# A decoder layer on one core: the feed-forward's first part cut into 6 and 10 blocks, copies issued by k-tiles

## The chip, the core and the metric

The kernel runs on one core of a Trainium2 chip. The metric is the device time of one execution in microseconds (us). Before the change it is 1711.41 us, the median of three runs (1711.17 to 1711.67).

## What is computed

One layer of a hybrid decoder for 256 prompt positions and 8 x 4 sample positions, 288 columns in all, with a model width of 2048 and a feed-forward width of 5632, in float32. Cut to the part in question:

```python
x1 = _layernorm(ALPHA * x + mixed @ w_out, ln1_g, ln1_b)

a, b = jnp.split(x1 @ w_up, 2, axis=-1)
a, conv_ffn_new = _causal_dwconv(a, conv_ffn_prev, w_conv_ffn)
y = _layernorm(ALPHA * x1 + (jax.nn.silu(a) * b) @ w_down, ln2_g, ln2_b)
```

Ahead of it stand one large input projection, a gated convolution, windowed attention over the prompt and over key/value caches, and two branch projections. The caches are also outputs: most of their rows are copied unchanged from input to output.

## The kernel before, in words

Features lie on the partitions in blocks of 128, the 288 positions in the columns. Every product is 128 output features by 288 positions, summed over k-tiles of 128 inputs. Operands are split into a high and a low float32r part, and a k-tile takes three matmuls (lines 245 to 247): high weight by high input, high weight by low input, low weight by high input. A product over 16 k-tiles has 48 matmuls.

`product` (its text is below) takes the next weight block from `w_ready` and calls `prepare` for the one after it. `prepare` loads a block of `weight_list` into `wst` (three buffers) by a DMA on SP's queue, and `half_block` splits it by eight k-tiles at a time: ACT casts to `whi`, DVE subtracts to `wlo` (four buffers each, line 251). Behind some loads it issues `copy_rest`, one of 84 copies of cache rows, 1 MB each, from input to output; before the change behind loads 20, 23, 27, 30, ..., that is 3 in 10 loads. The scheduler orders the instructions of every engine by a simulation of its own when the program is built.

The feed-forward runs over three parts of 16, 16 and 12 blocks (`THIRDS`). For each block k of a part there are two products with the input x: the first (`pa`) goes through the convolution (`conv_in`, `conv` at line 775) and silu (line 1083), the second (`pb`) is multiplied onto it (`gated`, lines 798 to 803), and the result is split into `gh[:, k]` and `gl[:, k]` (tiles `yah` and `yal`). Then 16 products of the part's own k-tiles with `w_down` follow, whose results are added into `dd`, the residual.

Part 0 is special. When it starts, the mean and the deviation of the first layer norm are only just known, so x still holds the values before normalising, times the gain. Its products therefore take `x_gb`, x with two more columns that carry gain and offset (290 columns), and `normed` (lines 1052 to 1055) finishes each result with the deviation `n1.r` and with `n1.nmr`. Beside it, in each of its 16 blocks, one of the 16 blocks of `dd` is normalised: two instructions on POOL (lines 1097 and 1098) and one on ACT (line 1099), held behind that block's `last_rows` (lines 787 and 788). In part 0's down-projection each `dd` block is split anew into x (`xh`, `xl`), then multiplied by ALPHA and added to the product (line 1116). From part 1 on x is normalised, and the products take 288 columns.

Of the kernel before, what the change touches and what calls it, by code (L numbers as in the profile page):

```python
# [12 lines left out]
AF = mybir.ActivationFunctionType  # L13
ALU = mybir.AluOpType
# [3 lines left out]
P = 128  # L18
D = 2048
KD = D // P  # L20
# [11 lines left out]
KF = FF // P  # L32
HK = KD // 2
THIRDS = (16, 16, 12)
NG, NH = 3, 4
DIL = (1, 4, 16)
BAND = 128
# [65 lines left out]
def layer_kernel(ctx: ExitStack, tc: tile.TileContext, ins, outs):  # L103
# [34 lines left out]
        return ap.bitcast(F32)  # L138


    loads = [0]
    w_load = [None]
    steps_on = [False]
    no_sync = mybir.DependencyInfo(mybir.DependencyClass.NoSync, mybir.DependencyReason.DATA)
# [9 lines left out]
    def copy_rest(after):  # L154
        if copies:
            behind(sp.dma_start(*copies.pop()), after)
# [10 lines left out]
    def weight_list():  # L167
        for b in range(3, NB_QKV + 3 * KD):
            yield ins["w_in"][b], KD
        for gate, w, nk in ((0, "w_a", KD), (KD, "w_b", NH)):  # L170
            for i in range(KD):
                yield ins["w_in"][NB_QKV + 3 * KD + gate + i], KD
                yield ins[w][i], nk
        for i in range(KD):
            yield ins["w_out"][i], KD
        f = wd = 0
        for nf in THIRDS:
            for _ in range(2 * nf):
                yield ins["w_up"][f], KD
                f += 1  # L180
            for _ in range(KD):
                yield ins["w_down"][wd : wd + nf * P * P].rearrange("(p c) -> p c", p=P), nf
                wd += nf * P * P

    w_left = weight_list()

    def prepare():
        src, nk = next(w_left, (None, 0))
# [6 lines left out]
        for k0 in range(0, nk, HK if loads[0] == 1 else nk):  # L195
            k = slice(k0, k0 + (HK if loads[0] == 1 else nk))
            d = sp.dma_start(st[:, k, :], src[:, k])
        n = loads[0]
        w_load[0] = d
        if n >= 20 and n % 10 in (0, 3, 7):  # L200
            copy_rest(d)
        w_ready.append([half_block(st, k0, min(HK, nk - k0)) for k0 in range(0, nk, HK)])

    last_mm = [None]
# [855 lines left out]
    f = 0  # L1060
# [3 lines left out]
    ident_r = sb(big, [P, P], "v_s", F32R)  # L1064
    act.copy(ident_r, ident)
    sums = []
    for part, nf in enumerate(THIRDS):
        gh = sb(big, [P, KD, T], "yah", F32R)
        gl = sb(big, [P, KD, T], "yal", F32R)
        for k in range(nf):  # L1070
# [18 lines left out]
                gated(gf, y, pb)  # L1089
            last_split = split(gh[:, k], gl[:, k], gf)  # L1090
            f += 1
            if part == 1:
                next(factors, None)
            if part == 0:

                with tc.issue_after(i_rows.ins):
                    pool.tensor_tensor(dd[:, k], dd[:, k], n1.r, ALU.mult)
                    pool.tensor_tensor(dd[:, k], dd[:, k], n1.nmr, ALU.add)
                act.activation(dd[:, k], dd[:, k], AF.Identity, bias=n1.at(n1.b, k), scale=n1.at(n1.g, k))
        if f == KF:  # L1100
            sp.dma_start(outs["o_cf"].rearrange("p (k r) -> p k r", k=KF), cf)
        if f == KF:
# [218 lines left out]
```

## Time and profile before

| | |
|---|---|
| median of three runs | 1711.41 us |
| the profiled execution: span from first to last instruction | 1709.3 us |
| the median of the runs less that span | 2.1 us |
| PE busy | 1700.4 us (99%) |
| DVE busy | 1194.6 us (70%) |
| ACT busy | 939.0 us (55%) |
| POOL busy | 387.1 us (23%) |
| DMA mean rate | 255 GB/s |

A time of its own beside the span is not listed for the profiled execution; it is one of the program's executions, and the runs stand 2.1 us above its span. The busy times say how long an engine had at least one instruction under way; a matmul counts with its whole way through the array, so that neighbours overlap. Part 0's up-projection runs from about 917 to 1105 us, its down-projection to about 1199.

### The profile page before, as it was taken

To read this page: it belongs to the slowest core of one execution; us is meant where nothing else is said; L and a number is where in the kernel's file an instruction comes from. 1 tells how busy PE (TensorE), PEld (TensorE's weight loads), DVE (VectorE), ACT (ScalarE), POOL (GpSimd) and SP (SyncE) were. 2 spreads that over 40 slices of the span, in tenths; PEclk is the share of its full clock that TensorE was granted. 3 is DMA by queue.
4 is the path that set the end of the run, shared out by engine and by line. 5 is a ranking of instruction groups with operands and counts; after the bars stand their busy time and mean duration, and the time that the engine had idled before them with its cause. 6 is when DMAs were issued, how large, how long until landed. Compare 5 with 4: busy or idle time off the path is not lost.

```text
span 1709.3 us, 34306 instructions
## 1 busy us (share of the span) xinstructions
PE 1700.4 (99%) x14138; PEld 1695.1 (99%) x14138; DVE 1194.6 (70%) x1575; ACT 939.0 (55%) x1657; POOL 387.1 (23%) x507
## 2 busy tenths in 40 slices
PE   9999999999999999999999999999999999999998
PEld 9999999999999999999999999999999999999997
DVE  5577898978887765455788887855686554555575
ACT  5578886645566564444546555543555443344454
POOL 1123332202222120011453332300111100011164
PEclk9999999999999999999999999999999999999999
DMA  8787886667778886677766666665666666666663
GB/s 295 289 299 311 333 320 251 227 260 278 268 290 341 319 313 248 225 255 258 273 232 227 230 246 227 232 233 222 228 232 256 222 231 237 247 224 234 218 243 133
DMA packets 59212, 436.16 MB, mean 255 GB/s; under 512 B 7664, under 2 KB 11504, under 8 KB 19312
## 3 DMA queue, kind: packets, MB, share of 16 engines
q1 hardware_dynamic: 57616, 429.85, 67.6%
q10 hardware_dynamic: 1440, 4.13, 0.7%
q8 instruction: 110, 1.80, 0.4%
q14 instruction: 46, 0.38, 0.1%
HBM read 427.50 MB, written 94.53 MB: 305 GB/s over the span
## 4 chain that ended last, share of the span: by engine, by line
PE 99%; DVE 0%; DMA 0%; ACT 0%; SPq 0%; issue 0%; DVEq 0%; ACTq 0%
PE acc L245 32%; PE acc L247 32%; PE acc L246 32%; PE acc L333 1%; PE att L478 0%; DMA wst<-in_w_in 0%; PE acc L437 0%; DVE yah L983 0%; PE att L597 0%; DVE ybh L957 0%; PE att L893 0%; PE att L896 0%; ACT cache L954 0%; DVE cache L965 0%; DVE cache L966 0%; DVE cache L989 0%
## 5 line engine op out<-in xcount | busy, mean ns | idle before, releaser
L251 DVE TENSOR_TENSOR wlo<-wst,whi 128x1024 fp32r<-128x1024 f32 (+1 forms) x578 | 739.5, 1282 | 404.0 <-ACT whi L251 401.1
L251 ACT CAST whi<-wst 128x1024 fp32r<-128x1024 f32 (+1 forms) x578 | 588.9, 1021 | 689.0 <-PE acc L246 613.4
L245 PE MATMUL acc<-xh,whi 128*128 128x288 f32 (+1 forms) x3216 | 921.1, 286 | 0.0
L246 PE MATMUL acc<-xl,whi 128*128 128x288 f32 (+1 forms) x3216 | 920.3, 286 | 0.0
L247 PE MATMUL acc<-xh,wlo 128*128 128x288 f32 (+1 forms) x3216 | 920.3, 286 | 0.0
L245 PEld LDWEIGHTS acc<-xh,whi 128*128 128x128 f32 x3216 | 607.8, 189 | 1.4 <-issue 1.4
L247 PEld LDWEIGHTS acc<-xh,wlo 128*128 128x128 f32 x3216 | 607.8, 189 | 0.0
L246 PEld LDWEIGHTS acc<-xl,whi 128*128 128x128 f32 x3216 | 607.8, 189 | 0.0
L247 PE MATMUL acc<-yah,wlo 128*128 128x288 f32 x1216 | 347.7, 286 | 0.0
L246 PE MATMUL acc<-yal,whi 128*128 128x288 f32 x1216 | 347.7, 286 | 0.0
L245 PE MATMUL acc<-yah,whi 128*128 128x288 f32 x1216 | 347.6, 286 | 0.0
L246 PEld LDWEIGHTS acc<-yal,whi 128*128 128x128 f32 x1216 | 229.8, 189 | 0.0
L247 PEld LDWEIGHTS acc<-yah,wlo 128*128 128x128 f32 x1216 | 229.8, 189 | 0.0
L245 PEld LDWEIGHTS acc<-yah,whi 128*128 128x128 f32 x1216 | 229.8, 189 | 0.0
L787 POOL COPY qk_s<-u 128x2 f32<-128x2 f32 x44 | 36.9, 838 | 535.2 <-ACT u L1080 412.5
L775 DVE SCALAR_TENSOR_TENSOR cy<-u,prm,cy 128x304 f32<-128x304 f32 x120 | 72.8, 606 | 6.0 <-ACT cy L773 2.8
L562 POOL TENSOR_TENSOR cache<-cache,dd 128x1024 f32<-128x1024 f32 x16 | 34.0, 2126 | 93.1 <-DMA cache<-in_cv 93.1
L251 ACT CAST yah<-ya 128x288 fp32r<-128x288 f32 x76 | 32.6, 429 | 24.4 <-DVE ya L803 8.2
L562 POOL TENSOR_TENSOR cache<-cache,qk_s 128x1024 f32<-128x1024 f32 x16 | 32.1, 2013 | 54.8 <-DMA cache<-in_ck 51.4
L768 POOL COPY u<-prm 128x16 f32<-128x16 f32 x60 | 43.1, 719 | 4.6 <-DMA prm<-in_prm 4.6
L846 POOL TENSOR_TENSOR ya<-ya,dd 128x288 f32<-128x288 f32 x16 | 13.7, 856 | 133.8 <-DVE ya L845 132.9
L560 ACT ACTIVATE cache<-cache,qk_s 128x128 f32<-128x128 f32 x128 | 40.7, 391 | 0.0
(230 smaller groups left out, 1187.2 us busy)
## 6 DMA issues: line engine op xcount, KB each, us to landing
wst<-in_w_in SPq DMA_DIRECT2D x112, 1024.0 KB, 5.1
wst<-in_w_up SPq DMA_DIRECT2D x88, 1024.0 KB, 4.9
wst<-in_w_down SPq DMA_DIRECT2D x32, 1024.0 KB, 4.9
cache<-in_ck SPq DMA_DIRECT2D x18, 1024.0 KB, 7.9
cache<-in_cv SPq DMA_DIRECT2D x18, 1024.0 KB, 8.7
wst<-in_w_a SPq DMA_DIRECT2D x16, 1024.0 KB, 5.4
wst<-in_w_out SPq DMA_DIRECT2D x16, 1024.0 KB, 5.0
wst<-in_w_down SPq DMA_DIRECT2D x16, 768.0 KB, 4.4
```

What stands on the lines that cost most here:

```text
L245: pe.matmul(out, hi[:, c, :], xh_k, start=k == 0, stop=False)
L246: pe.matmul(out, hi[:, c, :], xl_k, start=False, stop=False)
L247: last_mm[0] = pe.matmul(out, lo[:, c, :], xh_k, start=False, stop=k == nk - 1)
L251: return act.copy(hi, src), dve.tensor_tensor(lo, src, f32(hi), ALU.subtract)
L333: i = pe.matmul(o[b], first_w(term == 2, b, k), xk, start=k == 0 and term == 0, stop=k == KD - 1 and term == 2,)
L560: behind(act.activation(o[:, a, b], t[:, a, b], AF.Copy, scale=w[:, a, b : b + 1]), w_split[0])
L562: behind(pool.tensor_tensor(o, t, w.unsqueeze(3).broadcast_to([P, *n]), ALU.mult), w_split[1])
L768: pool.tensor_copy(tail[:, :, 0:2], prm[:, state : state + 2 * NB].rearrange("p (b r) -> p b r", b=NB))
L775: dve.scalar_tensor_tensor(y, u[:, i : i + YW], prm[:, w0 + i : w0 + i + 1], y, ALU.mult, ALU.add)
L787: pool.tensor_copy(dst[:, 0:2], u[:, SEQ : SEQ + 2])
L846: pool.tensor_tensor(m, m, ma[:, i], ALU.add)
```

## The change

`PARTS` has four entries: which third of `w_down`, its first k-tile in that third, and the number of blocks. The first third of 16 blocks is done as 6 and then 10. The weight arrays stay as they are laid out; a down-projection load of the first two parts takes 6 or 10 of a row's 16 k-tiles. In the first part, which is now of 6 blocks, each block normalises two or three blocks of `dd` (2, 3, 3, 2, 3, 3). The steps of the second norm's factors stay with the 16 blocks of the second third (`part == 2`). `copy_rest` is now called when 49 k-tiles have been loaded since the last copy, counted from load 20 on.

```diff
+PARTS = (0, 0, 6), (0, 6, 10), (1, 0, 16), (2, 0, 12)
+N_COPY = 49
...
-        f = wd = 0
-        for nf in THIRDS:
+        f = 0
+        for third, k0, nf in PARTS:
             for _ in range(2 * nf):
                 yield ins["w_up"][f], KD
                 f += 1
+            n = THIRDS[third] * P
+            wd = sum(THIRDS[:third]) * KD * P * P
             for _ in range(KD):
-                yield ins["w_down"][wd : wd + nf * P * P].rearrange("(p c) -> p c", p=P), nf
-                wd += nf * P * P
+                block = ins["w_down"][wd : wd + n * P].rearrange("(p c) -> p c", p=P)
+                yield block[:, k0 * P : (k0 + nf) * P], nf
+                wd += n * P
...
-        n = loads[0]
         w_load[0] = d
-        if n >= 20 and n % 10 in (0, 3, 7):
-            copy_rest(d)
+        if loads[0] >= 20:
+            to_copy[0] += nk
+            if to_copy[0] >= N_COPY:
+                to_copy[0] -= N_COPY
+                copy_rest(d)
...
-    for part, nf in enumerate(THIRDS):
+    for part, (_, _, nf) in enumerate(PARTS):
...
-            if part == 1:
+            if part == 2:
                 next(factors, None)
             if part == 0:
-                with tc.issue_after(i_rows.ins):
-                    pool.tensor_tensor(dd[:, k], dd[:, k], n1.r, ALU.mult)
-                    pool.tensor_tensor(dd[:, k], dd[:, k], n1.nmr, ALU.add)
-                act.activation(dd[:, k], dd[:, k], AF.Identity, bias=n1.at(n1.b, k), scale=n1.at(n1.g, k))
+                for i in range(k * KD // nf, (k + 1) * KD // nf):
+                    with tc.issue_after(i_rows.ins):
+                        pool.tensor_tensor(dd[:, i], dd[:, i], n1.r, ALU.mult)
+                        pool.tensor_tensor(dd[:, i], dd[:, i], n1.nmr, ALU.add)
+                    act.activation(dd[:, i], dd[:, i], AF.Identity, bias=n1.at(n1.b, i), scale=n1.at(n1.g, i))
```

The built program shows what this moves. At the end of part 0's last block, ACT had in a row before (the lines of the changed kernel are 10 or 11 higher):

```order
L1083 ACTIVATE cy_13503<-cy_13503 128x304
L1099 ACTIVATE dd_10045<-dd_10045,prm_182 128x288
L251 CAST whi_13645<-wst_13643 128x1024
L251 CAST yah_11185<-ya_13567 128x288
L251 CAST xh_91<-dd_10045 128x2x144
```

and has now:

```order
L261 CAST whi_12168<-wst_12166 128x768
L1062 COPY wgb_12091<-acc_12041 128x2
L1093 ACTIVATE cy_12030<-cy_12030 128x304
L1110 ACTIVATE dd_10044<-dd_10044,prm_182 128x288 x3
L261 CAST yah_11184<-ya_12090 128x288
L261 CAST xh_91<-dd_10044 128x2x144 x3
L261 CAST whi_12196<-wst_12194 128x768
```

The last cast into `yah` has three instructions on `dd` ahead of it, where it had one, and the cast of the fourth down block's weights moved ahead of all.

On POOL the same block had one pair:

```order
L787 COPY qk_s_11181<-u_13491 128x2
L788 COPY qk_s_11181<-u_13491 128x16
L1097 TENSOR_TENSOR dd_10045<-dd_10045,cache_10046 128x288
L1098 TENSOR_TENSOR dd_10045<-dd_10045,cache_10046 128x288
L766 MEMSET u_14783 128x2
```

and has three, all first halves ahead of all second halves:

```order
L797 COPY qk_s_11180<-u_12018 128x2
L798 COPY qk_s_11180<-u_12018 128x16
L1108 TENSOR_TENSOR dd_10044<-dd_10044,cache_10045 128x288 x3
L1109 TENSOR_TENSOR dd_10044<-dd_10044,cache_10045 128x288 x3
L776 MEMSET u_12761 128x2
```

On PE the first down products of part 0 now begin with 15 matmuls (five k-tiles) each of `acc_12116`, `acc_12144` and `acc_12172`; then the fourth product and the first use of the sixth k-tile stand so:

```order
L255 MATMUL acc_12200<-yah_11184,whi_12168 128x288
L256 MATMUL acc_12200<-yal_11185,whi_12168 128x288
L255 MATMUL acc_12116<-yah_11184,whi_12037 128x288
L255 MATMUL acc_12144<-yah_11184,whi_12112 128x288
L255 MATMUL acc_12172<-yah_11184,whi_12140 128x288
L257 MATMUL acc_12200<-yah_11184,wlo_12169 128x288
L256 MATMUL acc_12116<-yal_11185,whi_12037 128x288
L257 MATMUL acc_12116<-yah_11184,wlo_12038 128x288
```

Ahead of the first row are six more matmuls of `acc_12200`, so that 53 matmuls precede the first that reads the last block of `yah`. Before, that place came behind 45 matmuls of the first down product and 12 of the second.

## Rows read from the trace of the kernel before

**Rows 1.** The page: busy time, share of the span, instructions; granted clock in 40 slices.

```profile
PE 1700.4 (99%) x14138; PEld 1695.1 (99%) x14138; DVE 1194.6 (70%) x1575; ACT 939.0 (55%) x1657; POOL 387.1 (23%) x507
PEclk9999999999999999999999999999999999999999
```

**Rows 2.** The waits of PE: us in total, times, longest.

```profile
PE acc L263 <- DVE cy L260: 1.2, 1, 1.2
PE att L996 <- DVE ybh L957: 0.6, 1, 0.6
PE acc L333 <- ACT whi L300: 0.4, 1, 0.4
PE acc L978 <- DVE yah L983: 0.4, 1, 0.4
```

**Rows 3.** Windows of 160 us: busy us and (count) of PE, PEld, DVE, ACT, POOL.

```profile
940.00:1100.00 160.00, 160.00 (x1300) 160.00 (x1299) 131.06 (x192) 93.69 (x163) 54.23 (x81) 1.00 0.64 232
1210.00:1370.00 160.00, 160.00 (x1309) 160.00 (x1308) 112.02 (x193) 82.07 (x136) 22.91 (x55) 1.00 0.64 234
```

**Rows 4.** Timeline of PE, the first matmul of the first down product: start, us.

```profile
1105.37 0.29 PE L245 MATMUL acc<-yah,whi 128*128 128x288 f32 x1
```

**Rows 5.** Timeline of POOL in the last block of part 0.

```profile
1104.04 0.79 POOL L787 COPY qk_s<-u 128x2 f32<-128x2 f32 x1 [7.69 <-ACT u L1077]
1104.93 1.14 POOL L1097 TENSOR_TENSOR dd<-dd,cache 128x288 f32<-128x288 f32 x1
1106.15 0.92 POOL L1098 TENSOR_TENSOR dd<-dd,cache 128x288 f32<-128x288 f32 x1
1107.05 1.16 POOL L768 COPY u<-prm 128x16 f32<-128x16 f32 x1
```

**Rows 6.** Timeline of ACT there.

```profile
1107.10 0.63 ACT L1099 ACTIVATE dd<-dd,prm 128x288 f32<-128x288 f32 x1 [0.19 <-POOL dd L1098]
1110.01 0.43 ACT L251 CAST yah<-ya 128x288 fp32r<-128x288 f32 x1 [0.57 <-DVE ya L803]
```

**Rows 7.** Timeline of DVE there.

```profile
1106.53 1.62 DVE L251 TENSOR_TENSOR wlo<-wst,whi 128x1024 fp32r<-128x1024 f32 x1
1108.07 0.45 DVE L1054 TENSOR_TENSOR h<-acc,cache 128x288 f32<-128x288 f32 x1
1108.55 0.52 DVE L1055 SCALAR_TENSOR_TENSOR h<-cache,wgb,h 128x288 f32<-128x288 f32 x1
1109.18 0.49 DVE L800 SCALAR_TENSOR_TENSOR ya<-h,wgb,cy 128x256 f32<-128x256 f32 x1
1109.58 0.39 DVE L803 SCALAR_TENSOR_TENSOR ya<-h,wgb,cy 128x16 f32<-128x16 f32 x2
```

**Rows 8.** Groups by shape on DVE, 930 to 1112, then 1300 to 1410.

```profile
L775 DVE SCALAR_TENSOR_TENSOR cy<-u,prm,cy 128x304 f32<-128x304 f32 x32 | 25.6, 801 | 2.0 <-ACT cy L773 0.3
...
L775 DVE SCALAR_TENSOR_TENSOR cy<-u,prm,cy 128x304 f32<-128x304 f32 x16 | 8.5, 532 | 0.3
```

**Rows 9.** Line 1097 on POOL: duration ns, min/median/max, first and last start.

```profile
L1097 POOL TENSOR_TENSOR dd<-dd,cache x16: 792/1132/1139, 930.3 to 1104.9; 128x288 f32<-128x288 f32 x16
```

**Rows 10.** Groups by shape in part 0's down-projection, 1112 to 1200: DVE, then ACT.

```profile
L251 DVE TENSOR_TENSOR wlo<-wst,whi 128x1024 fp32r<-128x1024 f32 x30 | 36.8, 1225 | 26.3 <-ACT whi L251 26.3
L1116 DVE SCALAR_TENSOR_TENSOR dd<-dd,acc 128x288 f32<-128x288 f32 x16 | 7.3, 454 | 12.6 <-PE acc L247 12.6
L251 DVE TENSOR_TENSOR xl<-dd,xh 128x288 fp32r<-128x288 f32 x15 | 6.8, 454 | 0.0
...
L251 ACT CAST whi<-wst 128x1024 fp32r<-128x1024 f32 x31 | 32.4, 1046 | 52.4 <-PE acc L246 52.4
```

**Rows 11.** The page: DMA issues, count, KB each, median us to landing.

```profile
wst<-in_w_down SPq DMA_DIRECT2D x32, 1024.0 KB, 4.9
...
wst<-in_w_b SPq DMA_DIRECT2D x16, 256.0 KB, 2.7
```

**Rows 12.** Timeline of PE in the tail: its longest pause there, in brackets.

```profile
1700.42 0.40 PE L996 MATMUL att<-ybh,cache 128*128 128x288 f32 x1 [0.58 <-DVE ybh L957]
```

More of the change, by code (lines that the diff above doesn't have):

```diff
@@ L138, in f32 @@
         return ap.bitcast(F32)
-    loads = [0]
+    loads, to_copy = [0], [0]
     w_load = [None]
```

## The prediction

> **What bounds the kernel now.** The page comes first: PE is busy for 1700.4 of 1709.3 us, at a granted clock of 0.9 or more of full speed in every slice [rows 1]. A busy PE could still be a slow one, so the list of PE's waits is read next: it holds four waits, 2.6 us in all, two before or in the first three products (lines 263 and 333), two in the tail behind the last product (978 and 996) [rows 2]; none lies between. The third view is a count. In 160 us of the first part's up-projection PE issues 1300 matmuls of 290 columns, in 160 us of the second part's 1309 of 288 columns [rows 3]: 123.1 and 122.2 ns each, at the 2.4 GHz level. So PE streams without holes and the time is the number of matmuls times their columns. Only two things can move it: fewer columns, or a hole that the change tears.
>
> The profiled execution has a span of 1709.3 us; the runs' median of 1711.41 us is 2.1 us above it, for what lies around the span. I work out a difference and add it to the median. One part in 500, 3.4 us, is what a measurement here can tell from no change: faster ends at 1708.0, slower begins at 1714.8.
>
> **Term 1, columns.** A part-0 product reads x_gb (290 columns). Before, 16 blocks have two such products of 48 matmuls, now 6 have: 20 x 48 = 960 matmuls lose two columns. At 123.1 - 122.2 = 0.85 ns each [rows 3] that is **-0.8 us**, all of it on PE, so all of it in the time. The ten blocks also lose their normalising on DVE and ACT, which hides behind PE already: nothing.
>
> **Term 2, more and smaller products.** The count of matmuls stays (16 products of 48 become 16 of 18 and 16 of 30). Per product of 18 matmuls, 2.2 us at 122.2 ns, DVE has a split of 768 elements (three quarters of 1.225: 0.92), a split of x (0.45) and an addition (0.45), 1.8 us; ACT has 0.79 and 0.43 [rows 6, 10]. Both stay under PE, DVE by 0.4 us only. Of 30 matmuls, 3.7 us, DVE has 1.23 + 0.31 + 0.45 = 2.0. In the steady state these cost nothing; if DVE ran 20% slower here, PE would wait.
>
> **Term 3, where the parts meet.** The first down product needs the last block of gh. Before, it is the sixteenth of a product, and 45 + 12 = 57 matmuls, 7.0 us, stand ahead of its first use. Now it is the sixth. The order on PE shows the cover: 15 + 15 + 15 + 8 = 53 matmuls of four products go first, 6.5 us. Let T be the end of the up-projection (1105.37 before [rows 4]). I walk the change's order with durations from before.
> - u of the last block reaches POOL at T - 1.3 (1104.04), and the first dd instruction starts at T - 0.4 [rows 5]. One pair takes 1104.93 to 1107.07, 2.1 us. Before, a block has one pair; now the last one has three, and POOL runs them as three and three: 6 x about 1.03 = 6.2 us, so T + 5.7.
> - On ACT the three dd rows stand ahead of the last cast of yah, which is the move that matters. The last dd row takes 0.63, the cast 0.43 [rows 6]: T + 6.8 against T + 6.5, **0.3 us** late. DVE's own chain to ya (h, h, ya, ya: 1.9 us [rows 7], behind a split of 0.92 that starts at about T + 1.1) ends at T + 4, sooner, so POOL through ACT decides.
> - After it DVE has in its queue the split of yal (0.45), three of x and three additions (0.37 apart when back to back, 2.2), and only then the split of the fifth down block (0.92): T + 10.3. PE has 72 + 4 matmuls before that, T + 9.3 and the 0.3 lost: **0.6 us** more. Then DVE gains 0.4 us per product and the lag is gone.
>
> Bounds: if POOL always ran as in its shortest instance (0.79 [rows 9]), the cast ends at T + 5.4 and both waits vanish: 0. If all pairs take 2.14 and u comes 0.5 us late, as block 4's pairs hold ACT too, 1.1 and 0.6: 1.7 us. I take 0.9, since the shortest is one instance in 16 and the median is 1.13.
>
> How DVE and POOL meet is the unknown in this. With dd instructions beside it, cy on DVE takes 801 ns in the mean, without 532 [rows 8]; single instances of a split take 1.62 against 1.22 us [rows 7, 10]. So a dd instruction costs DVE about 0.4 us, half its own length. The walk above holds with 0.4 us.
>
> **Terms at zero.** At the 10-block part there are no dd instructions and no normalising, and the part of 12 made the same step before without any wait [rows 2]. The dd work itself, 32 POOL instructions, is the same, in 70 us rather than 190. The host's layout and the bytes are unchanged. SP issues 16 more loads (313, not 297) and 84 copies as before; one comes in 49 k-tiles rather than 3 in 10 loads (53 k-tiles for full blocks). Counted through the list of loads, a copy moves by at most 112 k-tiles (x 3 x 122.2 ns = 41 us), the last by 72, 26 us sooner. All are hidden by three wst buffers; no PE wait before names a DMA [rows 2]. The instructions after the last product stand in the same order, so the tail keeps its time.
>
> Sum: -0.8 + 0.3 + 0.6 = +0.1, **1711.5 us**.
>
> **Rivals.**
> *No hole.* POOL runs near 0.79 us, as DVE reads PSUM or idles part of the time: 1711.4 - 0.8 = 1710.6. For it: DVE waits for casts in this stretch. Against: 13 and more of 16 instances are long.
>
> *Loads come late (1712.5 to 1714).* 384 KB land, between 2.7 us for 256 and 4.9 for 1024 KB [rows 11], in about 3.1; a copy in front adds about 2.9 by the same slope. Then 0.79 and 0.92 for the splits: 7.7 us for a cycle of three products, 6.6. Each of the two copies behind loads of the 6-block down part could cost up to 1.1 us: 1711.5 + 2.2 = 1713.7. Against: the w_b stretch alternates products of 1.5 us without a PE wait, and DVE and ACT split a product ahead.
>
> *POOL and DVE take turns (the slower side).* Place: the last block of part 0. Between u and the cast DVE has 0.92 x 2 + 0.53 x 2 + 0.45 + 0.52 + 0.49 + 0.39 = 4.8 us [rows 7, 8], POOL 6 x 0.79 = 4.7. If none overlapped, the last dd instruction would end at T - 0.4 + 9.5 = T + 9.1, the cast at T + 10.1: 3.6 us late, with the 0.6 behind it 4.2, 1714.8. It decides from the point where turns take over 3.7 us, and if PE's clock fell to the 1.2 GHz level for as long as it stood, 1.8 us more: 1716.6. The clock did not fall in a pause of 0.58 us in the tail [rows 12]; longer ones the trace doesn't show. For it: a POOL copy of 16 elements that starts within a split takes 1.16 us, to the split's end [rows 5, 7]. Against: dd instructions end 0.92 us after their start beside a split that runs to 1.62.
> The Trainium skill, "SBUF — State Buffer", section "Who interferes with whom", says that DVE with two SBUF inputs and a GpSimd instruction share a port pair, which the first to issue holds for its whole instruction. The copy of 16 elements agrees; the 0.4 us by which DVE is late beside 0.9 to 1.1 us of POOL disagrees, so the sum goes by the rows; by the page it would be 1714.8.
>
> *The change brings what it looks like it could, time from DMA.* No PE wait on DMA exists to be removed [rows 2], so 3.4 us faster has no source.
>
> **How the numbers follow.** Forecast (1711.0 to 1712.3) 0.60; no hole (1710.4 to 1711.0) 0.19; loads late 0.12; turns 0.08; something unseen that gains 0.01. Leaving out turns and the upper half of late loads, the range is 1710.4 to 1713.4. Faster 0.01, within 0.2% 0.91, slower 0.08.
>
> **What would show it.** Right: 192 matmuls of 290 columns at L255 (before 512), two or three short PE waits, under 1.5 us in all, at the start of the first down part, on ACT's yah, whi and on wlo, none elsewhere; dd rows on ACT idle for POOL. Wrong in size: one wait of 3 us or more on yah there, or whi waiting for DMA in the down part. Wrong in kind: a PE wait at the 10-block part, or a changed tail.

## The result, and the profile after

The changed kernel takes **1713.13 us** in the median (1711.92 to 1714.98, 21 runs); before, beside it, 1711.05 us (1710.54 to 1711.67, 21 runs). The ratio is 1.0014, with a 95% interval of 1.0008 to 1.0021: slower by 2.1 us, where +0.1 was forecast. That is under the 3.4 us that the prediction took as the least that a run can tell, and inside its range; with so many runs it is told all the same, and the forecast of no change was wrong. The runs also scatter by 3.1 us, those of before by 1.1. A few executions in the sections below ran at a lower granted clock throughout (0.65 to 0.95; 1764.76 to 2546.88 us): the ranges leave them out, and the profile of the first set without copies, which is of one of them, isn't used. The profiled execution took 1712.88 us, with a span 1.8 us longer than that of before; its page:

```profile
span 1711.1 us, 34339 instructions
PE 1700.5 (99%) x14138; PEld 1694.2 (99%) x14138; DVE 1177.8 (69%) x1557; ACT 933.7 (55%) x1653; POOL 375.4 (22%) x507
PEclk9999999999999999999999999999999999999999
```

The clock is as before [rows 1]. The waits of PE, which had four entries [rows 2], now have three new ones:

```profile
PE acc L273 <- DVE cy L270: 1.2, 1, 1.2
PE acc L255 <- ACT yah L261: 1.0, 1, 1.0
PE att L1006 <- DVE ybh L967: 0.6, 1, 0.6
PE acc L343 <- DVE yal L318: 0.5, 1, 0.5
PE acc L257 <- DVE wlo L261: 0.4, 2, 0.2
PE acc L988 <- DVE yah L993: 0.4, 1, 0.4
PE acc L255 <- ACT whi L261: 0.3, 1, 0.3
```

Where they lie, the timeline of PE shows (start, us; in brackets the wait and what ended it). The first row is the first matmul of the first down product: T is 986.57 in this kernel.

```profile
986.57 0.29 PE L255 MATMUL acc<-yah,whi 128*128 128x288 f32 x1
...
992.94 0.29 PE L256 MATMUL acc<-yal,whi 128*128 128x288 f32 x1
994.18 0.64 PE L255 MATMUL acc<-yah,whi 128*128 128x288 f32 x3 [0.95 <-ACT yah L261]
...
996.74 0.29 PE L256 MATMUL acc<-yal,whi 128*128 128x288 f32 x1
997.05 0.39 PE L255 MATMUL acc<-yah,whi 128*128 128x288 f32 x1
997.28 0.29 PE L256 MATMUL acc<-yal,whi 128*128 128x288 f32 x1
997.74 0.39 PE L257 MATMUL acc<-yah,wlo 128*128 128x288 f32 x1 [0.17 <-DVE wlo L261]
...
1004.09 0.29 PE L256 MATMUL acc<-yal,whi 128*128 128x288 f32 x1
1004.63 0.39 PE L255 MATMUL acc<-yah,whi 128*128 128x288 f32 x1 [0.26 <-ACT whi L261]
```

I take a pause as the distance from one start to the next; without one it is 0.1225 us. There are five, all between 992 and 1021 us, in part 0's down-projection: 1.24 us for the last yah, 0.31 and 0.46 for the whi and wlo of the fifth down block, 0.55 for the whi of a late load, and 0.50 at 1020.05 for the wlo of another. After each pause one distance is 0.227, so a pause costs 0.10 more than its wait. Above 0.1225 that makes 1.22 + 0.73 + 1.00 = 2.95 us. The columns give 0.82 back (960 x 0.85 ns), and this execution's first 250 us hold 0.47 less pause than that of before: 2.95 - 0.82 - 0.47 = +1.7, against +1.8 of span.

Around the first pause, POOL, ACT and DVE, to compare with [rows 5 to 7]:

```profile
986.01 0.18 POOL L797 COPY qk_s<-u 128x2 f32<-128x2 f32 x1 [4.47 <-ACT u L1087]
986.37 3.25 POOL L1108 TENSOR_TENSOR dd<-dd,cache 128x288 f32<-128x288 f32 x3
989.58 3.49 POOL L1109 TENSOR_TENSOR dd<-dd,cache 128x288 f32<-128x288 f32 x3
993.11 0.63 ACT L1110 ACTIVATE dd<-dd,prm 128x288 f32<-128x288 f32 x1 [0.35 <-POOL dd L1109]
993.69 0.43 ACT L261 CAST yah<-ya 128x288 fp32r<-128x288 f32 x1
987.91 2.05 DVE L785 SCALAR_TENSOR_TENSOR cy<-u,prm,cy 128x304 f32<-128x304 f32 x2
989.88 1.56 DVE L261 TENSOR_TENSOR wlo<-wst,whi 128x768 fp32r<-128x768 f32 x1
991.36 0.45 DVE L1064 TENSOR_TENSOR h<-acc,cache 128x288 f32<-128x288 f32 x1
993.28 0.38 DVE L813 SCALAR_TENSOR_TENSOR ya<-h,wgb,cy 128x16 f32<-128x16 f32 x2
```

POOL's six dd rows take 6.7 us, where the walk had 6.2, and begin at T - 0.20, where it had T - 0.4. (u is later than that, T - 0.56 on POOL for T - 1.3, but the row that copies from it is shorter, 0.18 for 0.79.) And the cast of yah, at 993.69, has two things that end just before it: the last dd row on ACT at 993.74 (the rows overlap by 0.05) and ya itself on DVE, at 993.66. The row h on DVE, which takes the last product out of PSUM, starts at 991.36: T + 4.79. Which of the two holds the cast, and why h is so late, the trace doesn't settle by itself.

The loads, to compare with [rows 11], by the page: issues and median landing.

```profile
wst<-in_w_down SPq DMA_DIRECT2D x16, 384.0 KB, 4.0
```

And by the tile wst, the landing of the five 384 KB loads issued from 967 to 988 us, and of the eleven from 988 to 1014:

```profile
DMA to landing us min/median/max: 3.2/3.2/3.8
...
DMA to landing us min/median/max: 3.3/4.2/6.8
```

One by itself lands in 3.2 us, which the prediction interpolated as 3.1. In the down-projection, where three are issued within 3 us as buffers come free, they take 3.3 to 4.9; the two beside the first copy take 4.2 and 5.1, the last two, behind the second copy, 6.8 and 6.2.

### The profile page after: what moved, and what is told of

Its sections match the earlier page's. It is cut to its first block, busy times and chain, and to the rows that moved or that the text cites. A ratio compares the mean times of both kernels' runs of the same rounds, so it can differ in the third digit from the quotient of the medians.

```text
span 1711.1 us, 34339 instructions
## 1 busy us (share of the span) xinstructions
PE 1700.5 (99%) x14138; PEld 1694.2 (99%) x14138; DVE 1177.8 (69%) x1557; ACT 933.7 (55%) x1653; POOL 375.4 (22%) x507
## 4 chain that ended last, share of the span: by engine, by line
PE 96%; DMA 1%; DVE 1%; POOL 1%; ACT 1%; issue 0%; DVEq 0%; ACTq 0%
PE acc L255 31%; PE acc L257 31%; PE acc L256 31%; PE acc L343 1%; DMA wst<-in_w_down 1%; PE att L488 0%; POOL dd L1109 0%; POOL dd L1108 0%; DVE wlo L261 0%; ACT whi L261 0%; PE acc L447 0%; DMA dd<-in_w_in 0%; DVE yah L993 0%; PE att L607 0%; ACT dd L1110 0%
## 5 line engine op out<-in xcount | busy, mean ns | idle before, releaser
L261 DVE TENSOR_TENSOR wlo<-wst,whi 128x1024 fp32r<-128x1024 f32 (+2 forms) x594 | 739.4, 1250 | 402.5 <-ACT whi L261 399.9
L261 ACT CAST whi<-wst 128x1024 fp32r<-128x1024 f32 (+2 forms) x594 | 590.0, 999 | 683.7 <-PE acc L256 592.6
L785 DVE SCALAR_TENSOR_TENSOR cy<-u,prm,cy 128x304 f32<-128x304 f32 x120 | 69.2, 577 | 6.9 <-ACT cy L783 4.6
L808 DVE TENSOR_TENSOR ya<-cy,acc 128x256 f32<-128x256 f32 x108 | 28.6, 305 | 27.3 <-PE acc L257 27.0
```

The source lines that it names most:

```text
L261: return act.copy(hi, src), dve.tensor_tensor(lo, src, f32(hi), ALU.subtract)
L785: dve.scalar_tensor_tensor(y, u[:, i : i + YW], prm[:, w0 + i : w0 + i + 1], y, ALU.mult, ALU.add)
L808: dve.tensor_tensor(a, b, c, ALU.mult)
```

## The experiments

Two theories stood at the start, and both say something of each run: three losses of their own (yah, the fifth block's splits, late loads), or one cause behind all, the pacing of the copies or a chain in which one wait stands in for another. Each time below is a median, beside the kernel before on the same chip; "pauses" is the sum, in the profiled execution, of what PE's start-to-start distances have over 0.1225 us from 980 to 1040 us. In the versions with 6 and 10 blocks that holds the end of the first up-projection, the whole first down-projection (987 to about 1025) and the start of the next up-projection; the versions with 0 have none up to 1120 us either.

| version | us (runs) | before beside it | pauses |
|---|---|---|---|
| the change | 1713.13 (21) | 1711.05 | 2.96 |
| its parts, old pacing | 1715.63 (6) | 1710.91 | 4.80 |
| old parts, its pacing | 1710.71 (11) | 1710.91 | 0 |
| no copies in the stretch | 1712.35 (11), 1712.33 (8) | 1710.91, 1711.08 | 3.06 |
| w_down end to end | 1712.44 (11) | 1710.77 | 2.25 |
| dd dealt 3, 3, 3, 3, 3, 1 | 1715.48 (9) | 1710.91 | 5.08 |
| dd on ACT behind yah | 1716.81 (5) | 1710.77 | 6.05 |
| both of these | 1717.20 (5) | 1710.77 | 6.75 |
| dd behind yah, last block only | 1715.15 (7) | 1711.08 | 5.14 |
| that, and dealt 3, 3, 3, 3, 3, 1 | 1715.28 (10) | 1711.08 | 5.26 |
| that, and no copies | 1714.10 (11) | 1711.08 | 3.81 |
| no dd in part 0 | 1711.45 (11) | 1710.84 | 4.09 |
| two dd per block (four too early) | 1713.84 (11) | 1710.84 | 4.92 |
| that, and no copies | 1712.63 (11) | 1710.84 | 2.63 |
| two dd per block, four behind | 1715.38 (7) | 1710.69 | 6.51 |
| **parts of 8, 8, 16, 12** | **1709.99 (11), 1710.14 (11)** | 1710.77, 1710.69 | **0** |
| the same, old pacing | 1710.71 (11) | 1710.84 | 0 |

A profile is one execution: that of "no dd" is the slowest of its eleven (1713.87). The profiled executions, before's too, also have 4.6 to 5.5 us of pauses in their first 250 us, and what differs there lies in the first 8 us. The two of the parts of 8, one kernel, have 4.62 and 5.47, and their times differ by the same 0.85 us (1709.90 and 1710.75). So a difference of that size between single executions says nothing of an edit.

### One part of the change alone

```diff
-        if loads[0] >= 20:
-            to_copy[0] += nk
-            if to_copy[0] >= N_COPY:
-                to_copy[0] -= N_COPY
-                copy_rest(d)
+        n = loads[0]
+        if n >= 20 and n % 10 in (0, 3, 7):
+            copy_rest(d)
```

> The four parts, with the old pacing: five copies (at loads 173, 177, 180, 183, 187) fall among the sixteen small loads of part 0's first down projection, where the change has one behind load 179 and one behind 187. Theory (three losses: 1.2 us late yah cast, 0.75 us backlog of the first wlo, 1.0 us late loads that a copy shares the queues with): the wait for yah stays at about 1.0, the waits for whi and wlo of late loads grow from 1.0 to 1.5 to 3 us, so 1713.5 to 1715.5. Rival (the new pacing is what costs): 1711, as before the change.

1715.63 us (1715.06 to 1717.40), ratio 1.0031 (1.0018 to 1.0043). PE's waits for yah are as before this edit, those for whi and wlo have grown:

```profile
PE acc L255 <- DVE wlo L259: 1.0, 3, 0.5
PE acc L253 <- ACT whi L259: 1.0, 1, 1.0
PE acc L253 <- ACT yah L259: 0.9, 1, 0.9
```

So what the old pacing makes worse is the loads, with five copies among them: over before it is +4.7 against the change's +2.1. The new pacing saves 2.6 us of the loss that the split would make without it.

```diff
-PARTS = (0, 0, 6), (0, 6, 10), (1, 0, 16), (2, 0, 12)
+PARTS = (0, 0, 16), (1, 0, 16), (2, 0, 12)
```

> The three old parts with the new pacing of the copies. Theory: nothing there waits for loads, so 1711.0 to 1711.3, within 0.2 us of before, and PE's waits are the old four. Rival (the pacing itself costs, by another copy in the tail or at the end): 1712 to 1713.

1710.71, ratio 1.0000 (0.9991 to 1.0009), and PE's four old waits: the pacing by itself changes nothing that can be told.

### Late loads: copies, rows, bursts

```diff
-            if to_copy[0] >= N_COPY:
+            if to_copy[0] >= N_COPY and not 172 <= loads[0] < 190:
```

> The change without copies among loads 172 to 189; those that would have gone there follow behind loads 190, 191 and 192. Theory: the small loads land in 3.5 us or less and no whi or wlo of loads 180 to 189 is late: 1 us less, 1712.0 to 1712.4, and the times of one kernel lie closer together; the wait for yah stays at 1.0. Rival (loads of 3-KB rows land in 4 us without a copy too, and the three buffers of raw weights set the pace): 1712.8 to 1713.3.

1712.35 (1711.75 to 1713.22): 1.4 us over before where the change has 2.1, with half its scatter. A second set of the same version:

> The change without copies among loads 172 to 189 once more, for a profile at full clock (the first was taken while the chip granted 0.65 throughout). Theory: the pauses for yah (1.2) and the two behind it (0.3, 0.46) stay, those for whi and wlo of late loads (0.55, 0.50) are gone, landing of 384 KB 3.3 to 3.8 us. Rival: they stay, and landing is 4.0.

1712.33, 1.25 over before. Its profiled execution (1712.88) has two pauses by loads as well, 0.65 and 0.49, but they aren't the change's two. The first is the same, at 1004.58, with no copy near it. The one at 1020 is gone; the second stands in the first product behind the down-projection, on a 1024 KB load issued at 1015.50, just ahead of the postponed copies:

```profile
1024.90 0.39 PE L257 MATMUL acc<-xh,wlo 128*128 128x288 f32 x1 [0.21 <-DVE wlo L261]
```

The small loads from 988 to 1014 us land in 3.1 to 5.0 us:

```profile
DMA to landing us min/median/max: 3.1/4.0/5.0
```

Half of each theory: the longest landings (6.8) and the pause at 1020 were the copies'. In the medians the copies are worth 0.6 to 0.8 us, after what they cost where they went instead; the intervals of the two versions overlap (1.0008 to 1.0021 for the change, 1.0000 to 1.0018 here). The pause at 1004 stays, and so does a median landing of 4.0.

```diff
-            n = THIRDS[third] * P
-            wd = sum(THIRDS[:third]) * KD * P * P
+            n = nf * P
+            wd = sum(m for _, _, m in PARTS[: PARTS.index((third, k0, nf))]) * KD * P * P
...
-                yield block[:, k0 * P : (k0 + nf) * P], nf
+                yield block, nf
```

> The change with w_down laid out by the four parts, so that a block of six is 384 KB in one piece and its rows of 3 KB lie end to end, where in the change they lie 8 KB apart. Theory (the landing of 4.0 us is that of 128 rows of 3 KB, wherever they lie): no change, 1712.5 to 1713.3, median landing of 384 KB 3.8 to 4.1 us. Rival (the stride costs): landing 3.1 us or less, as the prediction interpolated, the late loads go, 1712.0 to 1712.3.

1712.44 (1711.72 to 1714.02), between the two expectations and not told from the change's scatter (1711.92 to 1714.98). One load by itself lands in 3.1 (3.2 in the change), and the median of the eleven of the stretch stays 4.2. But the burst of three on which the pause at 1004 hangs (issued from 998 to 1001) lands in 4.5, 4.2 and 3.6 us, where the change has 4.9, 4.6 and 4.0, and the pauses for late loads cost 0.28 us in this execution, not 1.00. Whether the layout did that, one execution each doesn't show. In both layouts a load lands later when two others or a copy are under way.

### The last yah: ACT's order, or DVE and POOL

```diff
-                for i in range(k * KD // nf, (k + 1) * KD // nf):
+                for i in range(DD[k], DD[k + 1]):
```

with DD = 0, 3, 6, 9, 12, 15, 16.

> The change with the sixteen blocks of dd dealt 3, 3, 3, 3, 3, 1 to the six blocks, so that the last has one in place of three. Theory: POOL is done with dd some 4.4 us sooner, the wait of the first down product for yah (1.2 us) goes, and part of the backlog of wlo (up to 0.75) with it; the late loads get up to 0.5 dearer, since the projection starts sooner: 1711.3 to 1712.3. Rival (the waits stand in for one another: what yah no longer holds up, the loads do): 1712.8 to 1713.3, with 2 us of waits for whi and wlo.

1715.48, 4.6 us over before and 2.5 more than the change, a clear miss. The timeline of ACT in the last block:

```profile
991.99 0.63 ACT L1111 ACTIVATE dd<-dd,prm 128x288 f32<-128x288 f32 x1 [1.36 <-POOL dd L1110]
992.53 0.81 ACT L262 CAST whi<-wst 128x768 fp32r<-128x768 f32 x1
```

With one dd row in that block the scheduler put it ahead of a whi cast, where it waits 1.36 us for POOL, and the cast, its wlo and PE's next weights wait behind it. There is a second loss. PE had four pauses from 990.87 to 996.66 (0.49, 0.46, 0.77 and 1.43), and then this, in the windows (busy us and count of PE, PEld, DVE, ACT, POOL, granted clock, DMA share, GB/s):

```profile
994.00:997.00 3.00, 1.47 (x9) 1.25 (x10) 2.36 (x7) 0.82 (x3) 0.00 (x0) 1.00 0.96 374
997.00:1001.00 4.00, 4.00 (x21) 4.00 (x20) 3.91 (x10) 3.37 (x7) 0.00 (x0) 0.57 0.26 98
```

The clock fell to the 1.2 GHz level after the pauses: 14 distances between matmuls are 0.24 us, which costs 14 x 0.117 = 1.6 us of the 5.08.

```diff
-                    act.activation(dd[:, i], dd[:, i], AF.Identity, bias=n1.at(n1.b, i), scale=n1.at(n1.g, i))
+                    i_dd = act.activation(dd[:, i], dd[:, i], AF.Identity, bias=n1.at(n1.b, i), scale=n1.at(n1.g, i))
+                    behind(i_dd, last_split[0])
```

> The change with each block's dd rows on ACT put behind that block's cast of yah, and nothing else. In the change the last of three dd rows ends at 993.74 and the cast starts at 993.69, but its input ya is written only by 993.66 too. Theory A (ACT's order holds the cast, as the prediction had it): the pause for yah falls from 1.2 to 0.2 or less, 1712.0 to 1712.3. Theory B (POOL's six dd operations slow DVE's cy, wlo and ya beside them, so ya itself is late): the pause stays at 1.1 to 1.2 and the time at 1713.0, within 0.3.

1716.81: in every block the three rows now stand ahead of the next block's whi, and all lateness moves there. With the deal above as well:

> The deal 3, 3, 3, 3, 3, 1 with the dd rows on ACT behind the cast of yah of their block. It lost 2.4 us on the change with that deal alone, where the one dd row of the last block went ahead of a whi cast on ACT and waited 1.36 us there for POOL. Theory B plus that reading: the whi cast no longer waits, POOL has one dd beside the last block and not three, so ya is 1 us or more sooner: pause for yah 0.3 or less, no stretch at clock 0.57, 1711.6 to 1712.2, what is left being late loads. Rival (the deal itself costs, by POOL's load in the blocks before): 1713 or more.

1717.20. Both miss both theories, since they change six blocks to test one. With `if k == nf - 1:` ahead of that last line only the last block is changed:

> The change with the three dd rows on ACT behind the cast of yah in the last block of part 0 alone (the run with this in every block put them ahead of whi casts of the blocks before, and is no test of the last one). Theory A (the three rows ahead of it on ACT hold the cast): pause for yah 0.3 or less instead of 1.2, 1712.0 to 1712.3. Theory B (ya itself is late, ended at 993.66 against the cast's start at 993.69; DVE runs beside six POOL operations): pause 1.1 to 1.3, 1712.8 to 1713.3.

The pause for yah stays, 1.22 us, with no dd row ahead of the cast. ACT waits for ya there, and what it was spared comes behind the cast:

```profile
993.78 0.43 ACT L261 CAST yah<-ya 128x288 fp32r<-128x288 f32 x1 [3.23 <-DVE ya L813]
994.12 1.66 ACT L1110 ACTIVATE dd<-dd,prm 128x288 f32<-128x288 f32 x3
995.69 1.08 ACT L261 CAST xh<-dd 128x288 fp32r<-128x288 f32 x3
996.67 0.83 ACT L261 CAST whi<-wst 128x768 fp32r<-128x768 f32 x1
```

That whi is 1.6 us later than in the change (996.67, not 995.10), so pauses of 0.98 and 0.84 follow and the clock falls (13 distances of 0.240 here): 1715.15 us, which neither theory had. Theory A, that the pause goes when ACT's order is changed, is out: DVE's chain alone makes it. This doesn't say that the three rows on ACT were harmless in the change; there they ended at 993.74, as late as ya did (993.66). The same with the deal, with and without copies:

> As pin_last, with the deal 3, 3, 3, 3, 3, 1, so that POOL has two operations of dd beside the last block in place of six. Theory B: from normed's first row to the cast 6.9 to 8 us (9.4 in the change, 6.9 in pin_early), pause 0.2 or less, the two pauses behind it (0.31 and 0.46) smaller too: 1711.2 to 1712.0, the late loads being left. Rival C (the block before, with its three dd, already puts DVE back, so the chain starts as late as before): pause 0.5 to 1.2, 1712.3 to 1713.3.

> As pin_last_early, without copies among loads 172 to 189. If the three losses (yah, the first wlo, late loads) are all, and each is mended: 1710.3 to 1711.0, no pause over 0.3. If the loads are late without copies too: 1711.3 to 1712.

1715.28 and 1714.10, times that no theory had. The chain from h of the last block's first product to the cast is shorter, 7.9 us against 9.4 in the change, but it starts 2.8 us later against T. That is rival C's mechanism: the blocks before set it.

### How late DVE runs in each block

Product j of part 0's twelve ends, as PE has no pause there, (11 - j) x 48 x 0.1233 us before T. The distance from there to DVE's row h for that product I call the lag. For the first product of blocks 2 to 6, and the last product of block 6 (block 6 alone starts among whi and wlo of the smaller loads):

| dd per block | 2 | 3 | 4 | 5 | 6 | last |
|---|---|---|---|---|---|---|
| before: 1 | 3.0 | 2.3 | 2.3 | 2.3 | 2.3 | 2.7 |
| the change: 2, 3, 3, 2, 3, 3 | 3.4 | 4.1 | 4.6 | 3.9 | 3.7 | **4.8** |
| 3, 3, 3, 3, 3, 1 | 4.9 | 5.7 | 6.2 | 6.7 | 6.5 | **7.2** |
| four too early: 6, 2, 2, 2, 2, 2 | 6.5 | 7.4 | 6.7 | 5.9 | 4.4 | **5.5** |
| 2, and four behind | 3.4 | 2.9 | 2.4 | 2.8 | 1.8 | **3.0** |
| none | 2.3 | 2.3 | 2.3 | 2.3 | 1.8 | 1.8 |
| parts of 8: 2 | 3.4 | 2.8 | 2.8 | 2.8 | 2.8 | 2.7 |

("Last" is the last product of part 0 in before and in the parts of 8 too.) In the full blocks of the change, one of three dd adds 0.5 to 0.7 us of lag, one of two takes 0.8 off. In the change the cast of yah ends 2.8 us after the last h, and PE needs it at T + 6.5: a lag over 3.7 us makes a pause.

What a block of three does, block 3 of the change shows (four rows), beside the same block with no dd (two rows, from a run below):

```profile
951.80 1.85 DVE L785 SCALAR_TENSOR_TENSOR cy<-u,prm,cy 128x304 f32<-128x304 f32 x2 [0.41 <-ACT cy L783]
953.57 1.82 DVE L261 TENSOR_TENSOR wlo<-wst,whi 128x1024 fp32r<-128x1024 f32 x1
956.09 0.63 ACT L1110 ACTIVATE dd<-dd,prm 128x288 f32<-128x288 f32 x1 [1.95 <-POOL dd L1109]
958.66 1.23 DVE L261 TENSOR_TENSOR wlo<-wst,whi 128x1024 fp32r<-128x1024 f32 x1 [0.49 <-ACT whi L261]
...
950.36 1.10 DVE L785 SCALAR_TENSOR_TENSOR cy<-u,prm,cy 128x304 f32<-128x304 f32 x2
952.02 1.23 DVE L261 TENSOR_TENSOR wlo<-wst,whi 128x1024 fp32r<-128x1024 f32 x1 [0.56 <-ACT whi L261]
```

From its first h to that of the next block (949.25 to 961.61) DVE takes 12.36 us, PE's two products 11.84. DVE is busy for 11.05 of them, without dd for 8.82, since its rows beside POOL's are longer; and it waits for ACT, whose dd rows stand idle for POOL. ACT's order counts by itself: with the same dd on POOL and the rows moved on ACT (1716.81 us) the lag of block 4 is 5.9, not 4.6. How much the longer rows on DVE add, no run separates.

```diff
-                for i in range(k * KD // nf, (k + 1) * KD // nf):
+                for i in range(2 * k, 2 * k + 2):
...
+                j = 2 * nf + i
+                if j < KD:
+                    for op, b in ((ALU.mult, n1.r), (ALU.add, n1.nmr)):
+                        pool.tensor_tensor(dd[:, j], dd[:, j], b, op)
+                    act.activation(dd[:, j], dd[:, j], AF.Identity, bias=n1.at(n1.b, j), scale=n1.at(n1.g, j))
```

> The change with two blocks of dd in each of part 0's six blocks, and the last four in the first four products of its down projection. In the traces the row h of DVE stands behind the end of its product by 2.3 to 2.7 us throughout before the change (one dd per block) and in the split 8, 8 (two), and by 3.4 rising to 4.8 in the change (three in four of six blocks), 4.9 rising to 7.2 with 3, 3, 3, 3, 3, 1. Theory L (three dd make a block take DVE, POOL and ACT longer than PE's 11.8 us, so the chain to yah starts later block by block): lag 2.7 in every block from the third on, yah's cast at T + 5.5 or sooner, no pause for it; the four late dd may cost DVE up to 0.4 us each beside POOL, hidden or not; late loads stay. 1711.0 to 1712.0. Rival (the lag has another cause, or the four late rows hold whi in the down projection): 1712.5 or more.

> two_each without copies among loads 172 to 189. If the yah chain and late loads are all that the change lost: 1710.2 to 1711.0, and the least of the four-part versions with 6 and 10.

1713.84 and 1712.63, with a pause of 1.56 us for yah in both: misses. The last four dd were meant for the down-projection, but nothing kept the scheduler from issuing them as soon as their inputs were there, in the first block. The lag of 7.4 after it, and how it shrinks block by block, is the table's best row all the same.

Without dd, the five lines of the loop over dd are taken out, so that the outputs behind it lack the normalising:

```diff
-                for i in range(k * KD // nf, (k + 1) * KD // nf):
...
-                    act.activation(dd[:, i], dd[:, i], AF.Identity, bias=n1.at(n1.b, i), scale=n1.at(n1.g, i))
```

> The change with the normalising of dd in part 0 left out (96 rows on POOL and ACT: sixteen blocks of two operations and one), so that o_y lacks it. Theory L: lag 2.3 to 2.7 in all six blocks, no pause for yah nor for the first whi and wlo; what is left is late loads, 0 to 1 us over the columns' gain: 1710.3 to 1711.3. Rival (a pause for yah comes from the short part itself, not from dd): pause 0.5 or more, 1711.8 or more.

1711.45 (1710.55 to 1713.87), 0.6 us over before and a little over the theory's 1711.3. The lag is flat, the last cast of yah starts at T + 3.8 (T + 7.1 in the change), and in the profile no pause for yah is left:

```profile
PE acc L257 <- DVE wlo L261: 1.2, 2, 0.7
PE acc L255 <- ACT whi L261: 1.2, 2, 1.0
```

What is left are loads, with their scatter: this execution has two copies among the small loads, and landings of up to 7.3 us there; its two longest pauses, 1.25 and 1.03, stand from 1023.4 on, in the first product behind the down-projection.

In the last trial the four stand where they were meant:

```diff
-                        pool.tensor_tensor(dd[:, i], dd[:, i], n1.nmr, ALU.add)
+                        i_dd = pool.tensor_tensor(dd[:, i], dd[:, i], n1.nmr, ALU.add)
...
+                    in_split.append(i_x)
+                j = 2 * nf + i - 6
+                if 2 * nf <= j < KD:
+                    with tc.issue_after(i_dd.ins):
+                        pool.tensor_tensor(dd[:, j], dd[:, j], n1.r, ALU.mult)
+                        pool.tensor_tensor(dd[:, j], dd[:, j], n1.nmr, ALU.add)
+                    i_late = act.activation(dd[:, j], dd[:, j], AF.Identity, bias=n1.at(n1.b, j), scale=n1.at(n1.g, j))
+                    behind(i_late, in_split[-2])
```

> Two blocks of dd in each of part 0's six blocks, and the last four on POOL behind the sixth block and on ACT behind the xh casts of products 5 to 8 of the down projection. In two_each, meant as this, the four were issued in the first block instead, so that it had six, and the lag of DVE's row h stood at 7.4 us from there and came down by 0.8 or 0.9 with each block of two. Theory L (a block of three adds lag, one of two takes it off): lag 2.7 to 3 us in the last block, cast of yah at T + 5.5 or sooner and no pause over 0.3 for it; the late loads stay, with the scatter: 1711.0 to 1712.3. Rival (the short part has a pause at yah whatever the deal): pause 0.5 or more, 1712.5 or more.

The lag is 3.0, as expected; the pause for yah, 0.54, and the time, 1715.38, are what the rival had, though not for its reason. POOL's eight late rows run beside DVE's chain, and here a lag of 3.0 is enough for a pause:

```profile
993.79 3.71 POOL L1132 TENSOR_TENSOR dd<-dd,cache 128x288 f32<-128x288 f32 x4
992.17 1.53 DVE L813 SCALAR_TENSOR_TENSOR ya<-h,wgb,cy 128x16 f32<-128x16 f32 x2
994.82 3.00 DVE L261 TENSOR_TENSOR xl<-dd,xh 128x288 fp32r<-128x288 f32 x3
```

In the change the three xl take 1.19 and these two ya rows 0.38 us. Here the three xl go at one per row of POOL (3.00 / 3 = 1.00, 3.71 / 4 = 0.93), pauses of 1.3 and 1.3 follow, and the clock falls as above. In none of these trials did six blocks take sixteen dd without a loss: more than two in a block put DVE back, and four behind them slow it where PE needs it.

### A version without these pauses

```diff
-PARTS = (0, 0, 6), (0, 6, 10), (1, 0, 16), (2, 0, 12)
+PARTS = (0, 0, 8), (0, 8, 8), (1, 0, 16), (2, 0, 12)
```

> Feed-forward in four parts of 8, 8, 16 and 12 with the change's pacing: 768 matmuls of 288 columns in place of 290 (0.65 us less than before), two dd per block, loads of 512 KB for products of 24 matmuls (2.94 us) in place of 384 KB for 18 (2.2 us). Theory: the last yah is needed after 8 of 8 blocks of three products (T + 8.8 us by the same walk, against T + 6.5), and it comes at T + 7 or sooner; a cycle of three loads has 8.8 us in place of 6.6, so no load is late: no wait in the two stretches, 1710.2 to 1710.6. Rival (small loads are late whatever the split, or the second part's loads of 512 KB are): 1711.5 to 1713.

> The split 8, 8, 16, 12 with the change's pacing once more, beside before: 1709.9 to 1710.2, 0.6 to 1.0 us under before, of which 0.65 are the 768 matmuls of two columns less.

1709.99 (1709.88 to 1710.72) and 1710.14 (1709.86 to 1710.75), against 1710.77 and 1710.69: 0.78 and 0.55 us faster, where 768 matmuls x 0.85 ns give 0.65. The intervals (0.9987 to 1.0005, both times) reach over 1; that two sets of 11 agree with the count of columns is what speaks for it. Against the change it is clear: the ranges don't meet. The old waits alone are left:

```profile
PE acc L273 <- DVE cy L270: 1.2, 1, 1.2
PE att L1006 <- DVE ybh L967: 0.6, 1, 0.6
PE acc L988 <- DVE yah L993: 0.4, 1, 0.4
```

Two dd per block keep the lag at 2.7, the last yah is needed later, and three products take 8.8 us, not 6.6, for loads that land in 4.7 (median).

> The split 8, 8, 16, 12 with the old pacing of the copies. Theory: a cycle of three loads has 8.8 us of PE work for landings of 4 to 8 us, so some loads may come late behind a copy, but far less than with 6 and 10, where the old pacing cost 2.5 us: 1710.0 to 1710.8. Rival (the new pacing is what makes the small loads bearable in this split too): 1711.5 or more.

1710.71 (1710.03 to 1711.02), and no pause in the down-projection either, though its loads land in up to 7.6 us: with the longer cycle the pacing isn't needed. The 0.6 us between the medians can't be laid to the pacing: the profiled execution has 5.12 us of pauses in its first 250 us, between the 4.62 and 5.47 of the two above.

## Why the prediction was wrong, point by point

**Columns, -0.8: right.** 192 matmuls of 290 columns are left on each of the three lines, and the parts of 8 bear out the price, within their interval: 0.78 and 0.55 us for 0.65.

**Where the parts meet, "0.3 us late": wrong, 1.22.** The step that failed is "DVE's own chain to ya ends at T + 4, sooner, so POOL through ACT decides". ya ends at T + 7.1, 3.1 us later, and the run with ACT's rows behind the cast shows that DVE's chain alone holds PE as long. The walk took DVE's position from the old kernel's last block, ahead of which every block had one dd. But the lag isn't a constant: the blocks with more dd had put DVE back to 3.7 us at the last block's first product, where it was 2.3 before. That is 1.4 of the 3.1. The rest came in the last block, where DVE's rows ran beside POOL's six: the two cy took 2.05 us (1.6 before), the split 1.56 (forecast 0.92), h to ya 2.3 (1.9).

The other chain was too short as well. POOL's six rows began 0.2 later and took 0.5 longer than in the walk, and the last dd row on ACT ended at T + 7.2, for T + 6.3. So two chains end within 0.1 us of each other, and by these times either would have held the cast; for POOL's through ACT no run shows it alone. The upper bound given for this wait, 1.1, has POOL's chain about right; that DVE's chain, which it leaves at T + 4, ends no later than POOL's is luck. A reading behind the rival with short rows was off too: 4 of the 16 rows of line 1097 took 0.79 us, and 12 were long, not "13 and more".

**The fifth block's splits, 0.6: right,** 0.73 measured. Whether all of it hangs on the yah, as the walk had it, the runs don't show: without dd one of the two pauses is still there (0.31).

**Loads "hidden by three wst buffers": wrong.** This is the second step that failed: a term put at 0, measured 1.00 in the profiled execution. ("In the steady state these cost nothing" held for the work on DVE and ACT, not for the loads.) The sum was left without the rival that it had priced. That rival had the landing of one load right (3.1, measured 3.2) and of one behind a copy about so (6.0; 6.2 and 6.8 behind the second copy, 4.2 and 5.1 beside the first); what it lacked is that loads come in bursts, three within 3 us, and then land in 4.0 in the median, and in up to 5.0, without any copy. With the terms as measured in the profiled execution the sum is -0.8 + 1.2 + 0.7 + 1.0 = +2.1, the difference of the medians. The medians of the experiments divide it another way: the change has +2.1 over before and the version without dd +0.6, so dd is worth 1.5, and the loads 0.6 and the 0.8 that the columns give back, 1.4. Of the loads' share 0.6 to 0.8 is the copies'.

**Rivals.** *No hole* is out. *Loads late* (chance 0.12) is a third to a half of what happened and should have stood in the sum, with the scatter that it brings. *POOL and DVE take turns* is not the change's case: six POOL rows and DVE's chain took 6.7 us, not 9.5, and the clock stayed up. But its mechanism is real in part: in the last trial with two dd per block DVE's xl go at the pace of POOL's rows. The Trainium skill, "SBUF — State Buffer", section "Who interferes with whom", calls the port pair that DVE with two SBUF inputs shares with GpSimd an exclusive lock, which the first to issue gets for its whole instruction. The traces show the contention and not the lock for a whole instruction. The three xl go at one per POOL row, and so do the two cy of the change (2.05 us for two, POOL's rows there 1.08 each; 1.1 for two with no dd beside them). But one whole instruction after the other would take 0.79 and 0.40, 1.19 us, for POOL's shortest row and an xl, and the pairs take 0.93 to 1.00. The fall of the clock that this rival priced came too, in versions that were not the change's.

**What would show it.** The places were right (short waits at the start of the first down part, on yah, whi and wlo; no other), the count wrong: five and 2.95 us, not two or three under 1.5. Whi waiting for a DMA was named as the sign of wrong size, and that is what stands there.

## What to carry to other kernels

When a queue is given more work per block, don't start its walk from where the old kernel's rows stood: take the lag of each row behind the event that feeds it, block by block, and ask whether a block now takes longer than the bound engine needs for it. A loss then grows with the blocks and falls due at the first place where the slack is short, here the last block, just ahead of smaller products with smaller loads. Price a load by how many others are under way, not by its size alone; and where a scheduler orders the rows, an edit without an order of its own may land elsewhere.

## What the runs showed of the hardware that was not expected

- After each pause of the change, and nearly each in the other versions, the next distance between matmuls is 0.227 us instead of 0.1225, after 0.31 us as after 1.56.
- The clock falls to the 1.2 GHz level in six of the versions, each time behind several pauses; the sizes and places of the pauses don't decide it alone. The version with dd behind yah in the last block and the deal 3, 3, 3, 3, 3, 1 has distances of 0.47, 0.60 and 1.56 us from 990.5 to 995.6 and then a fall (first row); without copies the same three, within 0.01, are followed by none (second row). Nor is there a fall in the change.

```profile
996.00:1000.00 4.00, 4.00 (x22) 4.00 (x21) 3.61 (x10) 4.00 (x10) 0.00 (x0) 0.57 0.25 98
...
996.00:1000.00 4.00, 3.31 (x25) 2.88 (x24) 3.61 (x9) 4.00 (x10) 0.00 (x0) 1.00 0.00 0
```

- Loads of 384 KB land in 3.2 us by themselves, in 3.1 to 5.0 (median 4.0) when three are issued within 3 us without a copy, and in 4.2 to 6.8 beside a copy in the change. With rows of 3 KB end to end, not 8 KB apart, a single load lands 0.1 us sooner and one burst of three 0.3 to 0.4.
